# A decoder block on one core: small sums kept together, squares of x out of the head, no low parts on GpSimd after w_o, sums of activations one set later, a last group of 384 and 128 tokens

## The chip, the core and the metric

The kernel runs on one core of one Trainium2 chip. A core has a matrix engine (TensorE, "PE" in the profile; its weight loads are "PEld"), a vector engine (VectorE, DVE), a scalar engine (ScalarE, ACT), GpSimd (POOL), a sync engine that here only issues transfers (SP), and 16 DMA engines. The metric is the device time of one execution in microseconds (us).

## What is computed

One layer of a hybrid decoder on 512 tokens of width 2048, in f32. Six vectors of 2048 (shifts, scales and gates) come from a conditioning vector `c` through `w_ada`; the normed and modulated input goes through one wide matrix `w_in`; two token mixers (latent attention and a gated delta rule) are merged by sigmoid gates; `w_o`, a residual, a second norm, a SwiGLU layer of width 5632, a residual and the last norm follow.

```python
mod = c_act @ w_ada[l] + b_ada[l]
sh_a, sc_a, gt_a, sh_f, sc_f, gt_f = ...
h = _rmsnorm(x, norm_mix[l]) * (1.0 + sc_a) + sh_a
p = h @ w_in[l]
...
mix = (g_a * y_a + g_b * y_b) @ w_o[l]
x = x + gt_a * mix
h = _rmsnorm(x, norm_ffn[l]) * (1.0 + sc_f) + sh_f
gate, up = jnp.split(h @ w_gate_up[l], 2, axis=-1)
x = x + gt_f * ((jax.nn.silu(gate) * up) @ w_down[l])
...
return _rmsnorm(x, final_norm)
```

## The kernel before

**Numbers.** Every f32 operand of a matmul is split into two parts of fewer bits, `hi` (a rounding copy on ACT, L263) and `lo = raw - hi` (a subtraction, L264), and each product is three matmuls: hi·hi, hi·lo, lo·hi (the names `hh`/`hl`, `h2h`/`h2l`, `ah`/`al` are such pairs). So every weight that arrives from memory costs PE three passes, ACT one copy and DVE one subtraction of 128x1024 elements. `lo` usually runs on DVE; for every second unit of some sets (`lo_eng`, `k0 % 4 == 0`) it runs on GpSimd.

**Order.** The work is a list of units. A unit has a load (its raw tile, issued on SP), a split (hi and lo), its matmuls, and a `pre` and `post`. A driver runs the units in order; it splits two units ahead and loads four ahead. After each 12 matmuls (or their weight) it "pumps" the open chains: generators whose steps are put between the matmuls (`yield 2` skips a pump more). PE, POOL and SP keep the order in which the program was written; DVE and ACT are ordered by a scheduler, and an instruction waits for what stands ahead of it on its engine.

**The head.** For k = 0 to 15 (128 rows of `w_in` and of x at a time), `mod_sum` multiplies two 128x1024 tiles of `w_ada` (`rawm`) with c and adds up along the row into `parts` (L435), `mod_columns` turns the two numbers into the scale `s_mix` (three instructions on 128x1 elements, L439, L440, L442), `scaled_h` makes `hh` on ACT and `hl` on DVE from x and the scale, and 24 matmuls of 512 columns follow (`s`, eight PSUM tiles of 128 output rows each). In the same loop `square(k)` squares the tile of x on ACT (L455) and adds it to `x_sum` on GpSimd (`x_sum<-x_sum,sq`). Ahead of the loop PE runs `warm` matmuls whose result is not used.

**The first gate set.** After the head the set `ga` (`ga_...` in the rows) runs in units of 24 matmuls. The chain `x_statistics` puts four one-column matmuls on `x_sum` between them (`xss`, the sums over rows), then a chain of 11 tiny DVE operations for 1/sqrt (`rs`), `diag`, one matmul `rbc` that spreads the result over the partitions, and a copy `r_all`. From then on DVE rescales the tiles of x (L489). Meanwhile DVE works on more `rawm` tiles and the `lo` of each unit.

**The middle.** `w_o` runs in four sets: three over all tokens, the last one (`half_sets`) first for tokens 0 to 255 and then for 256 to 511. When a set is done the residual is added to the tiles `x2[h][q]` (half h of the tokens, rows 256q to 256q+255, as two blocks of 256 columns), they are squared (`squares`), and the squares are added up on GpSimd, but for the last two tiles of a half. `half_rstd` sums them with 12 one-column matmuls (`hss`; the trace has two records for each), takes 1/sqrt, and `hbc` spreads it. `h2_gen` makes the normed halves `h2f` and their parts. The first set of `w_gate_up`, `gu0`, follows the same way in two halves of 8 units, while the second half of `h2` is made beside its first half. `combine` builds sums and differences of the activations (`x5`, `x6`, `x7`, `x3`, L1632, and their parts) for a Strassen product over the 20 later sets; it runs as a chain beside the second half of `gu0`. The set after it, `gu_both(1)`, runs over both halves with 384 matmuls.

**The last group.** The last product of `w_down` (4 of 44 blocks of rows) runs with all weights in place, first for tokens 0 to 255 (8 units of 24 matmuls, each 256 columns wide, names `dnl`), then for tokens 256 to 511. After each unit the residual is added, the tile squared, and scaled by the final norm's column on ACT; after the eighth, `finished(h)` sums the squares (`hss`), takes 1/sqrt, spreads it (`hbc`), multiplies the eight tiles (L1932) and writes them out. For the second half nothing else is left to run beside this.

Of the kernel before, what the change touches and what calls it, by code (L numbers as in the profile page):

```python
# [15 lines left out]
P = 128  # L16
# [155 lines left out]
def block_kernel(ctx: ExitStack, tc: tile.TileContext, a: dict, out):  # L172
# [40 lines left out]
    def bc(ap, n):  # L213
# [223 lines left out]
    def mod_columns(dst, ks, b, norm=None):  # L437

        nc.vector.tensor_reduce(dst[:, ks], parts[:, ks, :], AX.X, ALU.add)  # L439
        nc.vector.tensor_tensor(dst[:, ks], dst[:, ks], b[:, ks], ALU.add)  # L440
        if norm is not None:
            nc.vector.scalar_tensor_tensor(dst[:, ks], dst[:, ks], 1.0, norm[:, ks], op0=ALU.add, op1=ALU.mult)  # L442
# [6 lines left out]
    def square(k):  # L449
# [5 lines left out]
        nc.scalar.activation(s[:], xT[k][:], AF.Square)  # L455
# [4 lines left out]
    def x_statistics():  # L460
        yield 2
# [96 lines left out]
    def head():  # L558
        box = [dict() for _ in range(KT)]
        wait = deque()  # L560
        out_ = [0]
# [33 lines left out]
        for k in range(KT):  # L595
# [5 lines left out]
            square(k)  # L601
# [681 lines left out]
    sums = [[None, []] for _ in range(2)]  # L1283

    def add_gated(h, k, ps, gate):

        d = half_of(x2[h][k // 2], k)
        nc.vector.scalar_tensor_tensor(d, ps, gate[:, k:k + 1], d, op0=ALU.mult, op1=ALU.add)

    def squares(st, tile_, last):  # L1290

        if st[0] is None:
            st[0] = S("xs")
            nc.scalar.activation(st[0][:], tile_[:], AF.Square)
            return
        s = S("sq")
        nc.scalar.activation(s[:], tile_[:], AF.Square)
        if last:
            st[1].append(s)
        else:  # L1300
            nc.gpsimd.tensor_tensor(st[0][:], st[0][:], s[:], ALU.add)

    def half_rstd(st):

        ps = PS("hss")
        sq = [st[0]] + st[1]
        for t in range(2):
            for i, s in enumerate(sq):
                for j in range(2):
                    mm(ps[:, t:t + 1], s[:, 256 * j + P * t:256 * j + P * t + P], ones[:, 0:1], start=i == 0 and j == 0,  # L1310
                       stop=i == len(sq) - 1 and j == 1)
        st[0], st[1] = None, []
        y = token_rstd(ps[:, 0:2], 2, 1.0 / D)
        diag = S("diag")
        for t in range(2):
            nc.vector.tensor_scalar(diag[:, tok(t)], ident, y[:, t:t + 1], None, op0=ALU.mult)
        return diag

    def spread(diag):
        ps = PS("hbc")  # L1320
        mm(ps[:, 0:256], ones[:], diag[:, 0:256], start=True, stop=True)
        return ps[:, 0:256]

    def wo_done(n):
        def done(ps):
            for j in range(4):
# [3 lines left out]
                if j % 2:  # L1330
                    for h in range(2):
                        squares(sums[h], x2[h][k // 2], False)
# [14 lines left out]
    def half_sets(name, loads, x, done):  # L1347
# [3 lines left out]
        def unit(h, k0):  # L1351
# [5 lines left out]
            def split():  # L1357
                box["w"] = halves(box.pop("raw"), 512, 2, nc.gpsimd if k0 % 4 == 0 else None)
# [467 lines left out]
    def ffn():  # L1826
        def gu0():
# [16 lines left out]
            def start():  # L1844
# [3 lines left out]
                xc.append(drv.add(combine()))  # L1848
# [36 lines left out]
        def last_dn():  # L1885
# [11 lines left out]
        def last_unit(h, q):
            box = {}

            def pre():  # L1900
                box["ps"] = PS("dnl")

            def one(j, k, n, wi, xi):
                f = 2 * q + j
                mm(box["ps"][:, 256 * j:256 * j + 256], wl[f // 4, k][wi][:, tok(f % 4)], aT[40 + k][xi][:, 256 * h:256 * h + 256],
                   start=j == 0 and k == 0 and n == 0, stop=k == 3 and n == 2, skip_group_check=True)

            mms = [lambda j=j, k=k, n=n, wi=wi, xi=xi: one(j, k, n, wi, xi)
                   for j in range(2) for k in range(4) for n, (wi, xi) in enumerate(((0, 0), (0, 1), (1, 0)))]

            def post():
                xt = x2[h][q]
                for j in range(2):
                    add_gated(h, 2 * q + j, box["ps"][:, 256 * j:256 * j + 256], gt_ffn)
                squares(sums[h], xt, q > 5)
                for k in (2 * q, 2 * q + 1):
                    nc.scalar.activation(half_of(xt, k), half_of(xt, k), AF.Copy, scale=n_out[:, k:k + 1])
                if q == 7:
                    drv.add(finished(h))
# [102 lines left out]
```

## Time and profile before

| | |
|---|---|
| time, median of 3 runs (lowest, highest) | 2840.56 us (2837.66, 2842.48) |
| the profiled execution: its time, its span, granted TensorE clock | 2836.89 us, 2834.8 us, 0.993 |
| PE busy, share of the span | 2789.9 us, 98% |
| PEld, DVE, ACT, POOL busy | 88%, 66%, 37%, 9% |
| DMA, mean over the span | 174 GB/s |
| after the last `dnl` matmul begins (2816.77) to the end | 18.0 us |

The time is taken on the device from outside the span, so it is 2.1 us longer than the span. The profiled execution is 3.7 us below the median of the runs. A matmul's row in the trace gives its start and a modelled end that overlaps the next ones; how fast PE goes is read from the distance of the starts. "Granted clock" is the share of full speed that the throttle gave PE. With PE busy for 98% of the span, what is left for a change to take are PE's waits, the stretches at half clock, the matmuls themselves, and the tail.

### The profile page before, as it was taken

To read this page: it belongs to the slowest core of one execution; us is meant where nothing else is said; L and a number is where in the kernel's file an instruction comes from. 1 tells how busy PE (TensorE), PEld (TensorE's weight loads), DVE (VectorE), ACT (ScalarE), POOL (GpSimd) and SP (SyncE) were. 2 spreads that over 40 slices of the span, in tenths; PEclk is the share of its full clock that TensorE was granted. 3 is DMA by queue.
4 is the path that set the end of the run, shared out by engine and by line. 5 is a ranking of instruction groups with operands and counts; after the bars stand their busy time and mean duration, and the time that the engine had idled before them with its cause. 6 is when DMAs were issued, how large, how long until landed. Compare 5 with 4: busy or idle time off the path is not lost.

```text
span 2834.8 us, 43579 instructions
## 1 busy us (share of the span) xinstructions
PE 2789.9 (98%) x17082; PEld 2488.0 (88%) x17082; DVE 1860.8 (66%) x3121; ACT 1039.9 (37%) x1429; POOL 244.4 (9%) x284
## 2 busy tenths in 40 slices
PE   8999999999999999999989999999999999999997
PEld 7788788788888888888989999999999998888887
DVE  8875666666868547873475888888888863223234
ACT  4333432543344343222463444444444442112123
POOL 2200011001000000001420000000000140030001
PEclk9999999999999999999999999999999999999998
DMA  9995555545646459884543443444344474363331
GB/s 329 317 374 187 159 178 175 171 149 155 187 142 204 164 182 322 274 291 140 170 136 103 134 137 117 137 134 134 123 132 134 149 251 166 112 212 115 97 104 60
DMA packets 307270, 493.12 MB, mean 174 GB/s; under 512 B 47124, under 2 KB 161972, under 8 KB 306936
## 3 DMA queue, kind: packets, MB, share of 16 engines
q1 hardware_dynamic: 258936, 413.88, 45.2%
q0 software_dynamic: 14256, 46.44, 4.6%
q10 hardware_dynamic: 33872, 30.03, 3.2%
q8 instruction: 133, 2.18, 0.3%
q14 instruction: 73, 0.60, 0.1%
HBM read 438.87 MB, written 51.39 MB: 173 GB/s over the span
## 4 chain that ended last, share of the span: by engine, by line
PE 48%; DVE 1%; DMA 1%; ACT 1%; issue 1%; DVEq 0%; ACTq 0%; SPq 0%
PE m L155 27%; PE dn L155 15%; PE gu L155 3%; PE dnl L155 2%; PE wo L155 1%; DMA raws<-in_w_gate_up_dram 1%; PE hss L155 0%; DMA raw<-in_w_down_dram 0%; ACT h2f L1605 0%; DVE h2l L240 0%; DVE x L1932 0%; ACT hi L263 0%; DVE h2f L1604 0%; ACT h2h L239 0%; DVE lo L264 0%
## 5 line engine op out<-in xcount | busy, mean ns | idle before, releaser
L264 DVE TENSOR_TENSOR lo<-raw,hi 128x1024 fp32r<-128x1024 f32 x322 | 394.7, 1228 | 459.0 <-ACT hi L263 446.6
L263 ACT CAST hi<-raw 128x1024 fp32r<-128x1024 f32 (+1 forms) x338 | 352.1, 1044 | 928.8 <-PE dn L155 254.8
L435 DVE CUSTOM_DVE_ANT_0 rawm<-rawm,cbc 128x1024 f32<-128x1024 f32 x192 | 239.0, 1254 | 146.4 <-DMA rawm<-in_w_mod_dram 145.9
L1701 ACT CAST hi<-sums 128x1024 fp32r<-128x1024 f32 x160 | 167.8, 1049 | 330.4 <-PE m L155 234.5
L155 PE MATMUL m<-h2h,lo 128*128 128x256 f32 x960 | 271.8, 283 | 1.4 <-DVE lo L1702 1.4
L155 PE MATMUL m<-h2h,hi 128*128 128x256 f32 x960 | 271.7, 283 | 0.0
L155 PE MATMUL m<-h2l,hi 128*128 128x256 f32 x960 | 271.7, 283 | 0.0
L1702 DVE TENSOR_TENSOR lo<-sums,hi 128x1024 fp32r<-128x1024 f32 x160 | 195.8, 1224 | 115.2 <-ACT hi L1701 115.2
L155 PE MATMUL dn<-ah,hi 128*128 128x512 f32 x640 | 249.2, 389 | 0.4 <-DVE g L1718 0.4
L155 PE MATMUL dn<-al,hi 128*128 128x512 f32 x640 | 249.0, 389 | 0.0
L155 PE MATMUL dn<-ah,lo 128*128 128x512 f32 x640 | 249.0, 389 | 0.0
L155 PEld LDWEIGHTS m<-h2h,lo 128*128 128x128 f32 x960 | 184.3, 192 | 1.6 <-DVE lo L1702 1.6
L155 PEld LDWEIGHTS m<-h2h,hi 128*128 128x128 f32 x960 | 184.3, 192 | 0.0
L155 PEld LDWEIGHTS m<-h2l,hi 128*128 128x128 f32 x960 | 184.3, 192 | 0.0
L1701 ACT CAST hi<-raws 128x768 fp32r<-128x768 f32 x160 | 133.4, 834 | 122.3 <-PE m L155 88.8
L1702 DVE TENSOR_TENSOR lo<-raws,hi 128x768 fp32r<-128x768 f32 x160 | 152.1, 951 | 5.4 <-ACT hi L1701 5.4
L155 PEld LDWEIGHTS dn<-ah,hi 128*128 128x128 f32 x640 | 120.1, 188 | 26.3 <-DVE g L1718 0.8
L155 PEld LDWEIGHTS dn<-ah,lo 128*128 128x128 f32 x640 | 120.1, 188 | 24.9
L155 PEld LDWEIGHTS dn<-al,hi 128*128 128x128 f32 x640 | 120.1, 188 | 24.7
L1693 DVE TENSOR_TENSOR sums<-sums,raws 128x256 f32<-128x256 f32 x320 | 134.2, 420 | 4.1
L1693 DVE TENSOR_TENSOR sums<-raws 128x512 f32<-128x512 f32 x160 | 109.9, 687 | 10.9 <-DMA raws<-in_w_gate_up_dram 8.2
L155 PE MATMUL wo<-mh,lo 128*128 128x512 f32 (+1 forms) x320 | 111.0, 347 | 2.5 <-POOL lo L155 2.5
(482 smaller groups left out, 7322.7 us busy)
## 6 DMA issues: line engine op xcount, KB each, us to landing
rawm<-in_w_mod_dram SPq DMA_DIRECT2D x192, 512.0 KB, 5.3
raws<-in_w_gate_up_dram SPq DMA_DIRECT2D x320, 256.0 KB, 3.0
raw<-in_w_in_dram SPq DMA_DIRECT2D x144, 512.0 KB, 4.5
raw<-in_w_down_dram SPq DMA_DIRECT2D x88, 512.0 KB, 3.8
raw<-in_w_o_dram SPq DMA_DIRECT2D x40, 512.0 KB, 4.5
rawa<-in_w_in_dram SPq DMA_DIRECT2D x32, 512.0 KB, 4.7
raw<-in_w_gate_up_dram SPq DMA_DIRECT2D x48, 256.0 KB, 3.1
a_dram<-ah POOLq DMA_DIRECT2D x40, 256.0 KB, 2.4
```

What stands on the lines that cost most here:

```text
L155: return self.tc.keep_in_program_order(f(*args, **kwargs))
L263: nc.scalar.copy(hi[:], raw[:])
L264: (lo_eng or nc.vector).tensor_tensor(lo[:], raw[:], hi[:].bitcast(F32), ALU.subtract)
L435: nc.vector.tensor_tensor_reduce(raw, raw, c, 1.0, 0.0, ALU.mult, ALU.add, parts[:, k, half:half + 1])
L1693: add = lambda o, x, y: nc.vector.tensor_tensor(o, x, y, ALU.add)
L1701: nc.scalar.copy(hi[:], src)
L1702: nc.vector.tensor_tensor(lo[:], src, hi[:].bitcast(F32), ALU.subtract)
```

## The change

1. In the head the sums of tile k+1 (`mod_sum`) may only be issued after the last of the three small operations of tile k, so the scheduler cannot put them between those.
2. `square(k)` leaves the head. `x_statistics` now makes the 16 squares itself, two at each pump beside the gate set, before `xss`; the squares keep program order on ACT, the additions stay on GpSimd.
3. `n_out` (the final norm's 16 columns) leaves the first small load and gets a load of its own on SP later.
4. The last set of `w_o` and `gu0` put every `lo` on DVE (before: half of them on GpSimd).
5. `combine` starts with `gu_both(1)` and not in `gu0`, and takes two pumps for each of its steps.
6. `squares` works on segments of tokens; in `w_o`'s last set the last two tiles are added on DVE, so `hss` has 4 matmuls where it had 12.
7. The last group works on tokens 0 to 383 (eight units of 24 matmuls of 384 columns) and then 384 to 511 (four units of 48 matmuls of 128 columns). `finished` for the first part starts two pumps later and gives four pumps between `hss` and `hbc`. The last two tiles' squares stay separate: `hss` of the first part has 18 matmuls, of the last 6.

```diff
 def prepare(k):
-            for half in range(2):
-                use(lambda: mod_sum(box[k], k, half))
-            mod_columns(s_mix, slice(k, k + 1), b_cols[:, 16:32], n_mix)
+            with tc.issue_after(last[0].ins) if last else nullcontext():
+                for half in range(2):
+                    use(lambda: mod_sum(box[k], k, half))
+            last[:] = [mod_columns(s_mix, slice(k, k + 1), b_cols[:, 16:32], n_mix)]
...
-            square(k)
...
     def x_statistics():
-        yield 2
+        for k in range(KT):
+            square(k)
+            if k % 2:
+                yield
+        yield
         ps = PS("xss")
...
     def load_scalars():
+        load(n_out[:], a["out_norm"])
...
-                box["w"] = halves(box.pop("raw"), 512, 2, nc.gpsimd if k0 % 4 == 0 else None)
+                box["w"] = halves(box.pop("raw"), 512, 2)
...
-                    squares(sums[h], x2[h][k // 2], True)
+                    squares(k // 2, HALF[h], nc.vector)
...
                 for name in ("x3", "x6", "x7", "x5"):
                     comb[q][name] = hilo(res.pop(name)[:], name)
-                yield
+                yield 2
...
-                              cols=slice(256 * h, 256 * h + 256), lo_eng=True, alone=True)
+                              cols=slice(256 * h, 256 * h + 256), alone=True)
...
-                xc.append(drv.add(combine()))
...
-        yield from gu_both(1)
+        yield from with_pre(gu_both(1), lambda: xc.append(drv.add(combine())))
...
-            for h in range(2):
-                for q in range(8):
-                    yield last_unit(h, q)
+            for q in range(8):
+                yield last_unit(FIRST, [2 * q, 2 * q + 1], 1)
+            for q in range(0, 8, 2):
+                yield last_unit(LAST, [2 * q + i for i in range(4)], 4)
+
+        FIRST, LAST = [(0, 0, 256), (1, 0, 128)], [(1, 128, 128)]
...
+            mms = [lambda i=i, k=k, m=m, wi=wi, xi=xi: one(i, k, m, wi, xi)
+                   for i in range(len(fs)) for k in range(4) for m, (wi, xi) in enumerate(((0, 0), (0, 1), (1, 0)))]
...
+                for q in range(fs[0] // 2, fs[-1] // 2 + 1):
+                    for seg in segs:
+                        squares(q, seg, nc.gpsimd if q < 6 else None)
...
+        def finished(segs):
+            more = segs is FIRST
+            if more:
+                yield 2
+            diag = part_rstd(segs)
+            if more:
+                yield 4
+            r = spread(*diag)
```

**DVE at the start, before.** `lo` is the first unit's; L439, L440 and L442 make the first scale `s_mix`, `rawm` (L435) are the sums of the next tile.

```order
L264 TENSOR_TENSOR lo_186<-raw_149,hi_185 128x1024
L439 TENSOR_REDUCE s_mix<-parts 128x1
L435 ISA rawm_151,parts<-rawm_151,cbc 128x1024
L435 ISA parts 128x1
L440 TENSOR_TENSOR s_mix<-s_mix,columns 128x1
L435 ISA rawm_153,parts<-rawm_153,cbc 128x1024
L435 ISA parts 128x1
L442 SCALAR_TENSOR_TENSOR s_mix<-s_mix,columns 128x1
L439 TENSOR_REDUCE s_mix<-parts 128x1
```

After, the same place:

```order
L264 TENSOR_TENSOR lo_187<-raw_150,hi_186 128x1024
L439 TENSOR_REDUCE s_mix<-parts 128x1
L440 TENSOR_TENSOR s_mix<-s_mix,columns 128x1
L442 SCALAR_TENSOR_TENSOR s_mix<-s_mix,columns 128x1
L435 ISA rawm_152,parts<-rawm_152,cbc 128x1024
L435 ISA parts 128x1
L488 SCALAR_TENSOR_TENSOR hl_183<-xT_148,s_mix,hh_182 128x512
L435 ISA rawm_154,parts<-rawm_154,cbc 128x1024
L435 ISA parts 128x1
```

The three small operations of the first tile now follow each other directly; the two sums of the next tile stand behind them.

**DVE in the gate set, before.** The end of the 1/sqrt chain (`rs`), `diag` for the matmul `rbc`, and the `lo` of the set's fifth unit:

```order
L435 ISA rawm_1033,parts<-rawm_1033,cbc 128x1024
L435 ISA parts 128x1
L232 SCALAR_TENSOR_TENSOR rs_1077<-rs_1077,rs_1075 128x4
L233 SCALAR_TENSOR_TENSOR rs_1076<-rs_1077,rs_1076 128x4
L231 TENSOR_TENSOR rs_1077<-rs_1076 128x4
L232 SCALAR_TENSOR_TENSOR rs_1077<-rs_1077,rs_1075 128x4
L233 SCALAR_TENSOR_TENSOR rs_1076<-rs_1077,rs_1076 128x4
L468 TENSOR_SCALAR diag_1089<-kc,rs_1076 128x128 x4
L264 TENSOR_TENSOR lo_1101<-raw_1038,hi_1100 128x1024
L435 ISA rawm_1044,parts<-rawm_1044,cbc 128x1024
L435 ISA parts 128x1
L435 ISA rawm_1095,parts<-rawm_1095,cbc 128x1024
```

After, the end of the same chain (`lo_1189` is the eighth unit's):

```order
L264 TENSOR_TENSOR lo_1189<-raw_1142,hi_1188 128x1024
L231 TENSOR_TENSOR rs_1213<-rs_1212 128x4
L435 ISA rawm_1148,parts<-rawm_1148,cbc 128x1024
L435 ISA parts 128x1
L232 SCALAR_TENSOR_TENSOR rs_1213<-rs_1213,rs_1211 128x4
L435 ISA rawm_1181,parts<-rawm_1181,cbc 128x1024
L435 ISA parts 128x1
L233 SCALAR_TENSOR_TENSOR rs_1212<-rs_1213,rs_1212 128x4
L472 TENSOR_SCALAR diag_1225<-kc,rs_1212 128x128 x4
L264 TENSOR_TENSOR lo_1249<-raw_1186,hi_1248 128x1024
L435 ISA rawm_1192,parts<-rawm_1192,cbc 128x1024
L435 ISA parts 128x1
```

Before, `diag` stood ahead of the `lo` of the set's fifth unit; now it stands ahead of that of the ninth. On PE `xss` moved from the start of the third unit to the middle of the sixth, and `rbc` from the end of the third to the middle of the seventh.

**ACT in the gate set, after.** The squares of x (L455), the copies `hi` of the units, and `r_all`:

```order
L455 ACTIVATE sq_1084<-xT_446 128x512
L455 ACTIVATE sq_1087<-xT_491 128x512
L263 CAST hi_1096<-raw_1046 128x1024
L455 ACTIVATE sq_1114<-xT_536 128x512
L455 ACTIVATE sq_1117<-xT_581 128x512
L455 ACTIVATE sq_1132<-xT_626 128x512
L455 ACTIVATE sq_1135<-xT_671 128x512
L263 CAST hi_1144<-raw_1094 128x1024
L455 ACTIVATE sq_1162<-xT_716 128x512
L455 ACTIVATE sq_1165<-xT_761 128x512
L263 CAST hi_1188<-raw_1142 128x1024
L263 CAST hi_1248<-raw_1186 128x1024
L476 COPY r_all_89<-rbc_1266 128x512
```

The last six squares stand behind the copy `hi` of the sixth unit (`hi_1096`), and the very last two behind that of the seventh (`hi_1144`); before, ACT had only `hi` copies, eight copies of results and `r_all` in this set.

**DVE in `gu0`, before.** `h2f` and `h2l` make the second half's normed activations, L1632 and `x3l` to `x5l` are `combine`:

```order
L1632 TENSOR_TENSOR x_2044_12195<-h2f_12186,h2f_12026 128x512
L1632 TENSOR_TENSOR x_2045_12197<-h2f_11660,x_2044_12195 128x512
L1632 TENSOR_TENSOR x_2046_12199<-h2f_11660,h2f_12026 128x512
L1632 TENSOR_TENSOR x_2047_12201<-x_2045_12197,h2f_11820 128x512
L264 TENSOR_TENSOR lo_12328<-raw_12131,hi_12327 128x1024
L240 TENSOR_TENSOR x3l_12204<-x_2047_12201,x3h_12203 128x512
L240 TENSOR_TENSOR x6l_12220<-x_2045_12197,x6h_12219 128x512
L1604 SCALAR_TENSOR_TENSOR h2f_12242<-x_1766_10260,s_ffn,hbc_12024 128x256 x2
L264 TENSOR_TENSOR lo_12423<-raw_12227,hi_12422 128x1024
L240 TENSOR_TENSOR h2l_12248<-h2f_12242,h2h_12247 128x512
L240 TENSOR_TENSOR x7l_12252<-x_2046_12199,x7h_12251 128x512
L240 TENSOR_TENSOR x5l_12268<-x_2044_12195,x5h_12267 128x512
```

After, the same unit of `gu0`:

```order
L1621 SCALAR_TENSOR_TENSOR h2f_12176<-x_1764_10258,s_ffn,hbc_12014 128x256 x2
L264 TENSOR_TENSOR lo_12238<-raw_12081,hi_12237 128x1024
L240 TENSOR_TENSOR h2l_12182<-h2f_12176,h2h_12181 128x512
L1621 SCALAR_TENSOR_TENSOR h2f_12216<-x_1766_10262,s_ffn,hbc_12014 128x256 x2
L264 TENSOR_TENSOR lo_12278<-raw_12121,hi_12277 128x1024
L240 TENSOR_TENSOR h2l_12222<-h2f_12216,h2h_12221 128x512
L1621 SCALAR_TENSOR_TENSOR h2f_12256<-x_1768_10266,s_ffn,hbc_12014 128x256 x2
L264 TENSOR_TENSOR lo_12318<-raw_12161,hi_12317 128x1024
L240 TENSOR_TENSOR h2l_12262<-h2f_12256,h2h_12261 128x512
L1621 SCALAR_TENSOR_TENSOR h2f_12296<-x_1770_10270,s_ffn,hbc_12014 128x256 x2
L264 TENSOR_TENSOR lo_12349<-raw_12201,hi_12348 128x1024
```

The rows of `combine` are gone from here; they stand behind the twenty-odd rows that end `gu0`, between the units of the next set. The `lo` of each unit, half of which were on GpSimd, now all stand here.

More of the change, by code (lines that the diff above doesn't have):

```diff
@@ L1281, in load_x2, with add_gated, view @@
                      a["xT"][256 * q:256 * q + 256, 256 * h:256 * h + 256].rearrange("(k p) n -> p k n", p=P))
-    sums = [[None, []] for _ in range(2)]
-    def add_gated(h, k, ps, gate):
-        d = half_of(x2[h][k // 2], k)
+    sums = {}
+    def add_gated(h, k, ps, gate, c0=0):
+        d = half_of(x2[h][k // 2], k)[:, c0:c0 + ps.shape[1]]
         nc.vector.scalar_tensor_tensor(d, ps, gate[:, k:k + 1], d, op0=ALU.mult, op1=ALU.add)
[L1290 to L1295, printed above, removed]
+    def view(tile_, seg):
+        return tile_[:].rearrange("p (k n) -> p k n", k=2)[:, :, seg[1]:seg[1] + seg[2]]
@@ L1296, in squares @@
+    def squares(q, seg, eng):
         s = S("sq")
-        nc.scalar.activation(s[:], tile_[:], AF.Square)
-        if last:
-            st[1].append(s)
-        else:
-            nc.gpsimd.tensor_tensor(st[0][:], st[0][:], s[:], ALU.add)
-    def half_rstd(st):
+        st = sums.setdefault(seg, [])
+        nc.scalar.activation(view(s, seg), view(x2[seg[0]][q], seg), AF.Square)
+        if st and eng is not None:
+            eng.tensor_tensor(view(st[0], seg), view(st[0], seg), view(s, seg), ALU.add)
+        else:
+            st.append(s)
@@ L1305, in half_rstd, with part_rstd @@
+    def part_rstd(segs):
         ps = PS("hss")
[L1306 to L1313, printed above, removed]
+        n = sum(seg[2] for seg in segs) // P
+        todo = []
+        for i in range(max(len(sums[seg]) for seg in segs)):
+            t0 = 0
+            for seg in segs:
+                if i < len(sums[seg]):
+                    v = view(sums[seg][i], seg)
+                    todo += [(t0 + t, v[:, j, tok(t)]) for t in range(seg[2] // P) for j in range(2)]
+                t0 += seg[2] // P
+        for i, (t, v) in enumerate(todo):
+            mm(ps[:, t:t + 1], v, ones[:, 0:1], start=i == 0, stop=i == len(todo) - 1, skip_group_check=True)
+        for seg in segs:
+            del sums[seg]
+        y = token_rstd(ps[:, 0:n], n, 1.0 / D)
@@ L1314, in half_rstd, with spread @@
         diag = S("diag")
-        for t in range(2):
+        for t in range(n):
             nc.vector.tensor_scalar(diag[:, tok(t)], ident, y[:, t:t + 1], None, op0=ALU.mult)
-        return diag
-    def spread(diag):
+        return diag, n * P
+    def spread(diag, n):
         ps = PS("hbc")
-        mm(ps[:, 0:256], ones[:], diag[:, 0:256], start=True, stop=True)
-        return ps[:, 0:256]
+        mm(ps[:, 0:n], ones[:], diag[:, 0:n], start=True, stop=True)
+        return ps[:, 0:n]
@@ L1892, in last_dn @@
                     yield weights.pop(0)
-            for h in range(2):
-                for q in range(8):
-                    yield last_unit(h, q)
[L1897 to L1919, printed above, removed]
-            return Unit(mms=mms, pre=pre, post=post)
@@ new lines, in finished @@
+        def finished(segs):
[5 more added lines that the diff above has]
+                yield 4
+            r = spread(*diag)
+            o = 0
+            for seg in segs:
+                h, c0, n = seg
+                rs = r[:, o:o + n].unsqueeze(1).broadcast_to([P, 2, n])
+                o += n
+                for q in range(8):
+                    v = view(x2[h][q], seg)
+                    nc.vector.tensor_tensor(v, v, rs, ALU.mult)
+                    (load if more or q % 2 == 0 else nc.scalar.dma_start)(
+                        out[256 * q:256 * q + 256, 256 * h + c0:256 * h + c0 + n].rearrange("(k p) n -> p k n", p=P), v)
+                    if more:
+                        yield
```

63 lines of the change are left out of this document (39 added, 24 removed).

## The prediction

> **What bounds the kernel now.** First the page's engine table, then the waits of PE, then windows of the stages that the change touches. A change of under 0.2% (5.7 us) is about what a measurement of this kernel cannot tell from none.
>
> The page's busy times, and the first of PE's waits (total, times, longest):
>
> ```profile
> PE 2789.9 (98%) x17082; PEld 2488.0 (88%) x17082; DVE 1860.8 (66%) x3121; ACT 1039.9 (37%) x1429; POOL 244.4 (9%) x284
> ...
> PE gu L155 <- ACT h2h L239: 5.9, 2, 5.0
> PE hbc L155 <- DVE diag L1316: 5.0, 3, 2.8
> PE s L155 <- ACT hh L483: 4.4, 1, 4.4
> PE rbc L155 <- DVE diag L468: 3.4, 1, 3.4
> ...
> PE wo L155 <- POOL lo L155: 2.5, 1, 2.5
> ```
>
> PE is the bound at 98%, so only its waits, its half-clock stretches, its own work and the tail count. All five waits are touched by the change. Windows (span, then PE, PEld, DVE, ACT, POOL busy with counts, granted clock, DMA share, GB/s):
>
> ```profile
> 14.60:21.40 6.80, 5.64 (x12) 4.08 (x13) 6.16 (x17) 3.86 (x5) 0.00 (x0) 0.50 1.01 375
> 15.76:35.76 20.00, 20.00 (x75) 15.93 (x76) 18.80 (x30) 8.65 (x12) 3.08 (x2) 0.86 0.97 360
> 105.80:127.20 21.40, 18.01 (x84) 14.59 (x82) 15.04 (x37) 4.85 (x6) 1.65 (x4) 1.00 0.95 335
> 127.20:130.70 3.50, 3.50 (x9) 2.40 (x8) 3.50 (x7) 1.64 (x2) 0.00 (x0) 0.51 0.98 336
> 135.00:160.00 25.00, 25.00 (x112) 20.70 (x111) 23.38 (x37) 7.60 (x10) 2.16 (x4) 1.00 0.95 322
> 1417.50:1424.30 6.80, 6.80 (x34) 6.80 (x33) 3.22 (x13) 2.34 (x4) 2.35 (x1) 0.50 0.52 164
> 1428.00:1477.00 49.00, 42.50 (x325) 41.60 (x324) 40.03 (x54) 30.79 (x49) 12.04 (x5) 0.93 0.45 141
> 1468.70:1475.50 6.80, 6.50 (x28) 6.21 (x29) 4.43 (x8) 1.96 (x4) 0.00 (x0) 0.50 0.36 117
> 1477.00:1524.00 47.00, 47.00 (x393) 46.93 (x392) 23.67 (x35) 16.50 (x25) 2.74 (x5) 1.00 0.28 90
> 2791.90:2794.50 2.60, 2.60 (x26) 2.60 (x25) 0.48 (x1) 0.00 (x0) 0.00 (x0) 1.00 0.00 0
> ```
>
> Three things to see. A wait of PE is often followed by a stretch at clock 0.50 that costs half its length again. DVE is as good as full in the head (18.80 of 20) and in the gate set (23.38 of 25), but half idle in `gu_both(1)` (23.67 of 47). In `gu0`'s second half (1428 to 1477) PE is busy for 42.5 of 49 us, with DVE at 40.
>
> **1. Head.** The rows of the first tile:
>
> ```profile
> 12.38 0.15 DVE L439 TENSOR_REDUCE s_mix<-parts 128x1 f32<-128x2 f32 x1
> 12.44 1.21 DVE L435 CUSTOM_DVE_ANT_0 rawm<-rawm,cbc 128x1024 f32<-128x1024 f32 x1
> 14.80 0.15 DVE L442 SCALAR_TENSOR_TENSOR s_mix<-s_mix,columns 128x1 f32<-128x1 f32 x1
> 14.99 0.72 ACT L483 ACTIVATE hh<-xT,s_mix 128x512 fp32r<-128x512 f32 x1 [3.78 <-DVE s_mix L442]
> 15.76 0.79 PE L155 MATMUL s<-hh,hi 128*128 128x512 f32 x1 [4.38 <-ACT hh L483]
> ```
>
> Two `rawm` sums lie between L439 (12.38) and L442 (ends 14.95). Now the three small ones follow each other: 12.38 + two steps of about 0.2 + 0.15 = 12.95, so `hh` and the first matmul come 2.0 us earlier, at 13.8. PE's idle time before it falls from 4.4 to 2.4 us, so the half-clock stretch from 14.6 (12 matmuls in 6.8 us) shrinks or goes: worth 0 to 2.4 us, I take 1.5. The head gives **-3.5** (-2 to -4.4), if supply keeps up; with DVE freed of what follows, it should. The extra load of 16 columns is one small transfer among 97% busy DMA engines: nothing that shows.
>
> **2. Squares in the gate set.** What a GpSimd addition does to DVE:
>
> ```profile
> 27.39 1.79 POOL L155 TENSOR_TENSOR x_sum<-x_sum,sq 128x512 f32<-128x512 f32 x1 [19.34 <-ACT sq L455]
> 27.95 2.31 DVE L435 CUSTOM_DVE_ANT_0 rawm<-rawm,cbc 128x1024 f32<-128x1024 f32 x1
> L155 POOL TENSOR_TENSOR x_sum<-x_sum,sq 128x512 f32<-128x512 f32 x15 | 25.7, 1713 | 68.7 <-ACT sq L455 68.6
> ```
>
> The same DVE instruction takes 1.21 alone and 2.31 beside the addition: 1.1 us per addition, 15 x 1.1 = 16.5 us. They move from the head into the gate set, whose DVE is just as full, four per unit. Its rows:
>
> ```profile
> 126.59 1.47 PE L155 MATMUL rbc<-diag,ones 128*128 128x512 f32 x2 [3.39 <-DVE diag L468]
> 131.21 1.22 DVE L264 TENSOR_TENSOR lo<-raw,hi 128x1024 fp32r<-128x1024 f32 x1
> 133.65 1.06 ACT L263 CAST hi<-raw 128x1024 fp32r<-128x1024 f32 x1 [3.14 <-DVE parts L435]
> 135.96 1.22 DVE L264 TENSOR_TENSOR lo<-raw,hi 128x1024 fp32r<-128x1024 f32 x1
> ```
>
> Before, this stage lost about 5.6 us of waiting around `rbc` plus 1.8 at half clock (127.2 to 130.7). DVE made a unit in 4.75 us (131.21 to 135.96), PE needs 24 x 0.223 = 5.4 (25 us for 112): a gain of 0.65 per unit, no cover for 4.4. The last two squares stand on ACT behind the seventh unit's `hi`, which waits for DVE (before: 133.65). I date that copy: the sixth unit's `lo`, 131.21 before, moves by +12 (11 additions), -3.2 (the 1/sqrt chain now comes later), -1.4 (two rescalings too), -1.9 (head's gain less three result copies now ahead of the first `hi`): 136.7; the copy 2.4 later, 139.1; two squares and two additions, `xss` at about 144.5. PE without any stall would be at its place at about 132. So 12.5 us are lost there; then `rbc` waits some 2 us for the 1/sqrt chain, which now has a `lo` and four sums in it, and half clock follows for 1 us more than the starved PE would notice. 15.5 against 7.4: **+8**. Bounds: +1 if the additions fall into the idle time of DVE (it has 6.4 us from 105.8 to 127.2), +20 if an addition blocks DVE for all its 1.71 us (15 x 1.71 = 25.7, less 5.6 of slack and cover). I take the middle since the measured pair says 1.1.
>
> **3. The middle.**
>
> - `lo` on DVE: 16 x 1.22 = 20 us more work (8 units of `w_o`'s last set, 8 of `gu0`), against 16 times at least the 1.1 of blocking that a shorter GpSimd operation made: about even for DVE, and the wait `wo<-POOL lo` of 2.5 goes (**-2.6** with the clock step behind it).
> - `combine` out of `gu0`: 16 subtractions and 16 `lo` parts of 0.68 = 22 us of DVE leave a stage with 40 of 49 busy. The `h2h` that PE waited for stood behind two `lo` and two of `combine`'s parts. The waits of 5.9 and their restarts are about 7.8, the half clock from 1468.7 costs 3: **-10.8**. They go to `gu_both(1)`, where DVE then has 23.7 + 22 = 46 of 47 us at most (part of it ran there already). If that cover is too thin, PE waits there: +1 to +11, taken as +1.5.
> - `hss` with 8 records where there were 24 (26 records in 2.6 us): two halves save 2 x 1.6, and the second one's half clock from 1417.5 (3 us) with its `hbc` wait of 0.9 probably goes; an added DVE addition on the path costs about 1: **-6**.
>
> Together **-18**, of which I count -17 since a next wait always stands behind the one removed (range -10 to -20).
>
> **4. The last group.** The only rows for matmuls of 384 and 128 columns are the attention scores':
>
> ```profile
> 879.88 0.34 PE L155 MATMUL sc<-knl,qnh 128*128 128x384 f32 x1
> 880.05 0.34 PE L155 MATMUL sc<-knh,qnl 128*128 128x384 f32 x1
> 872.78 0.28 PE L155 MATMUL sc<-knl,qnh 128*128 128x128 f32 x1
> 872.89 0.28 PE L155 MATMUL sc<-knh,qnl 128*128 128x128 f32 x1
> 2784.83 0.28 PE L155 MATMUL dnl<-al,wlh 128*128 128x256 f32 x1
> 2784.95 0.28 PE L155 MATMUL dnl<-ah,wll 128*128 128x256 f32 x1
> ```
>
> Starts lie 0.17, 0.11 and 0.12 apart. Before: 384 x 0.120 = 46.1. After: 192 x 0.173 + 192 x 0.111 = 33.2 + 21.3 = 54.5, **+8.4**: 128 columns cost almost what 256 do. `hss` of the first part grows to 36 records (+1.2), its `hbc` wait (1.5) goes with four pumps; a half-clock stretch after so many one-column matmuls is likely (24 of them had one at 1417.5 and none at 2791.9): +2.5 of at most 3.4.
>
> The Trainium skill ("TensorE: Matmul & The Clock Gate", Back-to-back issue gap) gives about 81 ns per 128-column matmul in a stream with weight loads, and 131 ns for 512 columns. By it the last part would take 192 x 0.081 = 15.6, estimated, so 5.8 less. The rows here show 0.11, and 0.223 for 512 columns, so I go by the rows. The same page (LDWEIGHTS) has 107 ns for 128 columns of weights, which is the spacing seen.
>
> The tail, now over 128 tokens and not 256:
>
> ```profile
> 2817.09 0.88 DVE L1288 SCALAR_TENSOR_TENSOR x<-dnl,gt_ffn,x 128x256 f32<-128x256 f32 x2 [2.00 <-PE dnl L155]
> 2818.06 0.63 ACT L1297 ACTIVATE sq<-x 128x512 f32<-128x512 f32 x1 [1.31 <-DVE x L1288]
> 2819.63 1.16 PEld L155 LDWEIGHTS hss<-ones,sq 128*128 128x128 f32 x8
> 2823.68 1.22 PE L155 MATMUL hbc<-diag,ones 128*128 128x256 f32 x2 [2.81 <-DVE diag L1316]
> 2825.01 4.87 DVE L1932 TENSOR_TENSOR x<-x,hbc 128x512 f32<-128x512 f32 x8 [1.38 <-PE hbc L155]
> DMA packets 2177, 2.11 MB, mean 118 GB/s; under 512 B 128, under 2 KB 2176, under 8 KB 2176
> ```
>
> After the square `hss` keeps 4 records of 16 (-1.5), square and `diag` halve (-0.5), `hbc` halves (-0.4), eight multiplications of 4.87 become about 2.8 (-2.0); the output halves in bytes at the same number of rows, so the last transfers end -0.5 to -1.5 sooner. **-5.3** (-4 to -6). The last group: 8.4 + 1.2 - 1.5 + 2.5 - 5.3 = **+5.3** (+3 to +9).
>
> **Sum.** -3.5 + 8 - 17 + 5.3 = -7.2 us. The profiled execution of 2836.9 would become 2829.7. It lies 3.7 below the median of the runs, so against that median, 2840.6, I forecast 2833.4.
>
> **Rivals.**
> - *The gate set eats it all (slower).* If an addition holds DVE for its whole 1.71 us, and the late `xss` and `rbc` starve PE on top, the stage loses 28 against 7.4 before: +21, and the sum is +6 or more: 2847. It decides from 1.4 us per addition on. For it: DVE has no idle time at all from 127.2 to 130.7, and ACT's order ties the last squares to a unit's `hi` that needs DVE. Against: the measured 1.1.
> - *`combine` only moves its waits.* `gu_both(1)` would lose the 10.8 that `gu0` gains: -7.2 + 9.3 = +2: 2842.7, no change. For it: 46 of 47 us of DVE. Against: PE there needs only one `lo` of 1.22 per 5.75 us, which is split two units ahead.
> - *The squares cost nothing new.* With DMA 95% busy and DVE idle for 6.4 us of the set's first 21.4, the additions may fall into gaps that DMA makes: +1 for +8, -14.2 in all: 2826.4.
> - *128-column matmuls run at their own width*, half of 0.120: 192 x 0.060 = 11.5, the last group 9.8 cheaper: 2823.6. Against: the `sc` rows. The skill's 81 ns would give 2827.6.
>
> **How the numbers follow.** The forecast's case 0.42, squares free 0.18, gate set eats it 0.15, `combine` moves 0.20, narrow matmuls quick 0.05. Faster by over 0.2% (under 2834.9): two thirds of the first, all of the second and the last: 0.50. Slower (over 2846.2): the third and a fifth of the fourth: 0.20. Within: 0.30. The first case alone spans 2827 to 2840. The range 2823 to 2847 leaves out the worst of the gate set and the sum of all good ends.
>
> **What would show it.** `s` at about 13.8 us; waits `xss<-POOL x_sum` of several us and an `rbc` wait; `rawm` rows of 2.3 between 115 and 150 us; no `wo<-POOL lo` and no wait of `gu` over 1 us, `gu0` at 46 to 47 us per 384 matmuls, DVE near full in `gu_both(1)`; `dnl` starts 0.173 and 0.111 apart; about 12.5 us from the last `dnl` to the end. The forecast is wrong if the gate set ends at the same distance from its start as before, if `gu` waits move one set on, or if the 128-column starts are not 0.11 apart.

## The result: 16.6 us slower; the last group alone lost 25 us

The changed kernel takes 2857.6 us (median of 4 runs, 2854.9 to 2859.5), the kernel before 2841.0 beside it: ratio 1.0059, 95% interval 1.0042 to 1.0077. The forecast was 2833.4, faster, with a range that ended at 2847. The profiled execution took 2859.5, its span 2857.7, that is 22.9 more than the one before. (The profiled execution after is the slowest of its four, the one before is faster than all four beside it, so the traces show some 6 us more than the medians.)

The engines, PE's waits and the clock by slices, from the page and the view of waits, after:

```profile
PE 2811.1 (98%) x17050; PEld 2510.7 (88%) x17050; DVE 1877.2 (66%) x3165; ACT 1042.9 (36%) x1453; POOL 209.9 (7%) x273
...
PEclk9999999999999999999999999999999999999996
...
PE xss L155 <- POOL x_sum L155: 11.8, 1, 11.8
PE hbc L155 <- DVE diag L1331: 6.8, 3, 2.6
PE k L155 <- DVE lo L264: 3.7, 1, 3.7
...
PE s L155 <- ACT hh L487: 2.4, 1, 2.4
...
PE hss L155 <- DVE sq L1308: 1.9, 1, 1.9
```

The waits of `gu` and of `wo` are gone, `s` has 2.4 where it had 4.4, `rbc` has none; new is `xss` with 11.8. The last slice's clock is 0.6 where it was 0.8. A page of busy times hides the main loss: PE is at 98% again, since matmuls at half clock count as busy.

Where the 22.9 us arose, from the starts of each stage's matmuls in the two traces:

| stage | before | after | difference |
|---|---|---|---|
| to the end of the head's `s` | 105.6 | 102.7 | -2.8 |
| gate set `ga`, to its end (`ga` to `q`) | 94.1 | 104.1 | +10.0 |
| up to `w_o` (a longer wait of `k`, 526 us) | 1028.6 | 1031.0 | +2.3 |
| `w_o` with the first half's `hss` | 182.5 | 180.1 | -2.4 |
| `gu0`, first half of tokens (30.6, 30.5), second (33.0, 23.0) | 63.6 | 53.6 | -10.0 |
| `gu_both(1)` | 46.4 | 46.1 | -0.4 |
| Strassen sets and `w_down` up to the last group | 1244.9 | 1246.2 | +1.3 |
| last group, first to last `dnl` | 50.8 | 77.8 | +27.0 |
| from there to the end | 18.0 | 16.0 | -2.1 |

Windows of the last group after (columns as before: span; PE, PEld, DVE, ACT, POOL busy; clock; DMA share; GB/s), and two rows of PE:

```profile
2797.29:2801.26 3.97, 3.97 (x38) 3.97 (x37) 0.74 (x2) 2.32 (x6) 0.00 (x0) 1.00 0.00 0
2807.60:2817.60 10.00, 10.00 (x48) 10.00 (x49) 3.43 (x18) 2.11 (x6) 0.72 (x1) 0.50 0.01 2
2819.20:2841.70 22.50, 22.50 (x108) 22.50 (x107) 9.67 (x24) 4.23 (x12) 2.92 (x4) 0.50 0.34 111
...
2801.26 6.24 PE L155 MATMUL hss<-ones,sq 128*128 128x1 f32 x36
2817.64 1.59 PE L155 MATMUL hbc<-diag,ones 128*128 128x384 f32 x2
```

The 128-column stream begins at full clock, 38 matmuls in the first 3.97 us (two of them at the edges of the window). The first part's `hss` follows, and from 2802.94 to the end the clock is 0.50: 48 matmuls in 10.0 us, 108 in 22.5, which is 0.21 each and not 0.111. Everywhere else in these two traces a half-clock stretch ahead of the tail ends after 3.4 or 6.8 us, or 13.7 in the starved gate set. This one lasts for the 54.8 us that remain.

### The profile page after: what moved, and what is told of

It reads as the page before. It is cut to its first block, busy times and chain, and to the rows that moved or that the text cites. A ratio compares the mean times of both kernels' runs of the same rounds, so it can differ in the third digit from the quotient of the medians.

```text
span 2857.7 us, 43631 instructions
## 1 busy us (share of the span) xinstructions
PE 2811.1 (98%) x17050; PEld 2510.7 (88%) x17050; DVE 1877.2 (66%) x3165; ACT 1042.9 (36%) x1453; POOL 209.9 (7%) x273
## 4 chain that ended last, share of the span: by engine, by line
PE 94%; DVE 2%; DMA 2%; ACT 1%; issue 1%; POOL 0%; ACTq 0%; SPq 0%; DVEq 0%; POOLq 0%
PE m L155 27%; PE dn L155 15%; PE gb L155 6%; PE wo L155 6%; PE v L155 4%; PE z L155 3%; PE gu L155 3%; PE ya L155 3%; PE yb L155 3%; PE q L155 3%; PE s L155 3%; PE dnl L155 2%; PE k L155 2%; PE ga L155 2%; PE qk L155 2%; PE ckv L155 2%
## 5 line engine op out<-in xcount | busy, mean ns | idle before, releaser
L264 DVE TENSOR_TENSOR lo<-raw,hi 128x1024 fp32r<-128x1024 f32 x338 | 418.3, 1240 | 452.8 <-ACT hi L263 439.4
L435 DVE CUSTOM_DVE_ANT_0 rawm<-rawm,cbc 128x1024 f32<-128x1024 f32 x192 | 241.2, 1269 | 153.6 <-DMA rawm<-in_w_mod_dram 153.2
L155 PE MATMUL wo<-mh,hi 128*128 128x512 f32 (+1 forms) x320 | 111.2, 347 | 0.0
```

The costliest lines, as they stand in the source:

```text
L155: return self.tc.keep_in_program_order(f(*args, **kwargs))
L264: (lo_eng or nc.vector).tensor_tensor(lo[:], raw[:], hi[:].bitcast(F32), ALU.subtract)
L435: nc.vector.tensor_tensor_reduce(raw, raw, c, 1.0, 0.0, ALU.mult, ALU.add, parts[:, k, half:half + 1])
```

## The experiments

**The last group.** Four kernels, each the changed one with one edit.

*a1_halves*: 256 and 256 tokens again.

```diff
-                yield last_unit(FIRST, [2 * q, 2 * q + 1], 1)
-            for q in range(0, 8, 2):
-                yield last_unit(LAST, [2 * q + i for i in range(4)], 4)
+                yield last_unit(FIRST, [2 * q, 2 * q + 1], 2)
+            for q in range(8):
+                yield last_unit(LAST, [2 * q, 2 * q + 1], 2)
-        FIRST, LAST = [(0, 0, 256), (1, 0, 128)], [(1, 128, 128)]
+        FIRST, LAST = [(0, 0, 256)], [(1, 0, 256)]
```

> The changed kernel with its last group back at 256 and 256 tokens (8 + 8 units of 24 matmuls of 256 columns); everything else of the change stays. Theory (the last group's half clock is the loss): matmuls of 256 columns keep the array full at half clock as well, so the clock comes back to 1.00 within 7 us of `hss`; the last group takes 51 us and not 78, the tail 2 us more: about 2833, below the kernel before. Rival (the loss sits in the other parts and the clock at the end is only a symptom): over 2845.

Measured: 2829.4 us (2827.3 to 2833.4), 0.9968 [0.9955, 0.9980] of the kernel before: faster than that, and 26 us less than the changed kernel by the two ratios (0.0091 x 2840). Its `hss` drops the clock as well, but 256 columns bring it back in one stretch:

```profile
2789.20:2792.70 3.50, 3.50 (x19) 3.50 (x18) 2.52 (x13) 0.76 (x2) 0.09 (x1) 0.51 0.00 0
2792.70:2809.00 16.30, 16.30 (x137) 16.25 (x136) 9.07 (x18) 8.41 (x17) 6.39 (x5) 1.00 0.39 131
```

*a4_late_hss*: the first part's chain 12 pumps later.

```diff
             if more:
-                yield 2
+                yield 12
             diag = part_rstd(segs)
```

> The changed kernel, with the chain of the first part started 12 pumps later and not 2, so that 150 matmuls of 128 columns run before any one-column matmul. Theory A (one-column matmuls drop the clock): the clock is 1.00 for these 16 us, starts 0.111 apart, and falls only at the late `hss`; the first part's end then lies in the tail: about 2850. Theory B (the stream drops it by itself): 0.50 within 3.4 to 7 us of the first 128-column matmul, ahead of any `hss`: 2860 or more.

Measured: 2857.0 (2852.9 to 2858.3), 1.0057 [1.0042, 1.0072]. The time lies between A's 2850 and B's 2860 and decides nothing, as the first part's multiplications now lie in the tail; the clock answers the question:

```profile
2797.50:2813.30 15.80, 15.80 (x144) 15.80 (x144) 3.24 (x12) 6.19 (x18) 2.19 (x3) 1.00 0.00 1
2814.70:2828.00 13.30, 13.30 (x63) 13.30 (x64) 2.47 (x14) 0.49 (x2) 0.64 (x1) 0.50 0.00 0
...
2813.45 6.75 PE L155 MATMUL hss<-ones,sq 128*128 128x1 f32 x36
```

Narrow matmuls keep full clock for 15.8 us, 144 in a row. `hss` begins at 2813.45, the clock falls at 2814.6, and the same stream then stays at 0.50. So theory B falls: the stream does not drop the clock, `hss` does.

*a3_push*: 24 matmuls of 512 columns behind `hss`.

```diff
             diag = part_rstd(segs)
             if more:
+                push = PS("push")
+                for _ in range(24):
+                    mm(push[:], wl[0, 0][0][:, tok(0)], aT[40][0][:], start=True, stop=True)
                 yield 4
```

> The changed kernel, with 24 matmuls of 512 columns, whose result is not used, put behind `hss` of the first part (10 us at half clock, 5.5 at full). Theory A (128 columns keep the clock that they find): the wide matmuls release the throttle after 3.4 to 6.8 us, and the rest of the 128-column stream runs at 0.111: saves some 13 us and costs 8: 2850 to 2854. Theory B (the stream drops the clock itself): the clock comes back and falls again within 7 us: 2860 to 2865. Theory C (the low clock at the end has another cause than how busy the array is): no return, 2866 to 2868.

Measured: 2849.6 (2847.3 to 2855.6), 1.0041 [1.0028, 1.0055]: 8 us less in the medians and 5 by the ratios than without this extra work (the intervals overlap), just below A's 2850 to 2854.

```profile
2805.30:2811.50 6.20, 6.20 (x16) 4.94 (x17) 2.46 (x14) 0.00 (x0) 0.00 (x0) 0.50 0.00 0
2815.50:2831.70 16.20, 16.20 (x144) 15.94 (x143) 10.55 (x28) 6.35 (x18) 3.66 (x5) 1.00 0.48 156
```

The wide matmuls bring the clock back after 6 us, and the narrow stream behind them (144 in 16.2 us) holds it to the tail. Theory C falls too: the same code at the same place runs at either clock, depending on what ran before it.

*a2_few_hss*: the last two squares added on DVE, 12 records of `hss` and not 36.

```diff
-                        squares(q, seg, nc.gpsimd if q < 6 else None)
+                        squares(q, seg, nc.gpsimd if q < 6 else nc.vector)
```

> The changed kernel, with the last two tiles' squares added on DVE too, so that `hss` of the first part has 12 records of one column and not 36. Theory A (one-column matmuls drop the clock, and a stream of 128 columns keeps whatever clock it finds): with 1.3 us of them and not 5 no window is idle enough, the clock stays 1.00, the 128-column starts stay 0.111 apart: about 2832 to 2835. Theory B (a stream of 128 columns drops the clock by itself, since its weight loads leave the array half idle): the clock falls to 0.50 within 7 us of the stream's start all the same: 2850 to 2855.

Measured: 2852.5 (2850.9 to 2856.5), 1.0046 [1.0031, 1.0061]: in time this is B's figure, and A's figure is missed.

```profile
2799.90:2801.20 1.30, 1.30 (x14) 1.30 (x13) 0.00 (x0) 0.00 (x0) 0.00 (x0) 1.00 0.00 0
2803.70:2833.40 29.70, 29.70 (x137) 29.09 (x137) 11.29 (x31) 6.34 (x18) 3.65 (x5) 0.50 0.26 85
```

With a4 beside it, A holds, but its figure for a window that is idle enough was wrong: 1.3 us of one-column matmuls among narrow ones were enough for the drop, and not in the profiled run alone: the granted clock of the four runs is 0.985 to 0.987, near the changed kernel's 0.984 to 0.985 and not a1's 0.991 to 0.993. (Among 256-column matmuls 0.9 us of them were not, e2 below.)

**Head, gate set, `combine`.** Four kernels on top of a1_halves (2829.4).

*d1_xss*: `xss` 36 matmuls later.

```diff
             if k % 2:
                 yield
-        yield
+        yield 4
         ps = PS("xss")
```

> On the last group of 256 and 256 tokens (2829.4): `xss` stands 36 matmuls (8.2 us at full clock) later on PE, in the seventh unit's second half; nothing else moves but what follows it. Theory A (PE waits 11.8 us at `xss` for a chain of 14 GpSimd additions of 2.06 us, while the weights' parts are ready): PE works through most of that time, the wait falls to 2 to 4 us and the time to 2821 to 2824. Theory B (DVE, slowed by the same additions, is the limit, and `xss` only the place where it shows): PE waits for `lo` instead, or for `rbc` later; less than 3 us gained, 2827 or more.

Measured: 2828.9 (2824.3 to 2830.1), 0.9964 [0.9951, 0.9977]: no difference from a1 that the runs can tell. In its profile the wait of `xss` fell and the gate set took 4.2 us less:

```profile
PE xss L155 <- POOL x_sum L155: 4.8, 1, 4.8
...
PE ga L155 <- DVE lo L264: 1.2, 2, 0.8
PE rbc L155 <- DVE diag L472: 1.0, 1, 1.0
```

Part of A's and part of B's: 7 us less at `xss`, 1.8 of them back at `ga` (0.4 in a1) and `rbc` (none in a1). That the rest did not reach the time fits a half-clock stretch of 6.8 us at 521.9, where a1 had none; nothing here shows that it would come in each run.

*d2_sqhead*: the squares back in the head, the tie kept.

```diff
-        for k in range(KT):
-            square(k)
-            if k % 2:
-                yield
-        yield
+        yield 2
         ps = PS("xss")
...
+            square(k)
             u, head_units[k] = head_units[k], None
             u.pre()
```

> On the last group of 256 and 256 tokens (2829.4): the squares of x and their additions are back in the head, `xss` at its old place; the small sums stay tied. If moving the squares is what cost 10 us in the gate set, and the tie alone gave the head's 2.8 us: the head ends at 102.7 to 103.5, the gate set as before the change, about 2819.5. Rival (the head's gain came from the squares leaving it): the head ends at 105 or later, 2822 or more. Second rival (the gate set is slow for another reason, such as the set's three result copies ahead of its first `hi`): no gain, 2829.

Measured: 2819.9 (2819.2 to 2821.0), 0.9935 [0.9918, 0.9951]: 9.5 us less than a1, as expected. In the profiles the head ends at 104.4, 1.6 us later than in a1 and between the expected 103.5 and the rival's 105: part of the head's gain did come from the squares. The gate set takes 13.8 less; `rbc`, which lost 3.4 us before the change, now waits 1.1:

```profile
PE s L155 <- ACT hh L483: 3.8, 1, 3.8
...
PE rbc L155 <- DVE diag L468: 1.1, 1, 1.1
```

*d4_comb0*: `combine` in `gu0` again, at its old pace (in `gu0`'s start `xc.append(drv.add(combine()))` and not at `gu_both(1)`; `yield` for `yield 2`).

> On the last group of 256 and 256 tokens (2829.4): `combine` is back in `gu0`'s second half, one pump for each step. If it was `combine` on DVE that made PE wait in `gu0`: the wait of `h2h` at about 5 us is back, with a half-clock stretch, 8 to 11 us slower: 2837.5 to 2840. Rival (the low parts on GpSimd made that wait, and they stay away here): within 3 us, 2829 to 2832.

Measured: 2837.5 (2833.0 to 2843.1), 8.1 more than a1. `gu0`'s second half takes 27.9 us for 23.0, with a wait of `h2h` again, 2.6 us and not 5, and clock 0.94:

```profile
1447.40:1474.80 27.40, 24.50 (x190) 24.10 (x189) 26.52 (x38) 16.91 (x25) 0.00 (x0) 0.94 0.56 173
...
PE gu L155 <- ACT h2h L239: 2.6, 1, 2.6
```

So `combine` made that wait, and 4.9 of the 9.1 us between the two spans lie where it was; the rest lies in half-clock stretches and waits elsewhere, outside the edit.

*d6_untie*: without the tie (the `with tc.issue_after...` line of `prepare` removed).

> On the last group of 256 and 256 tokens (2829.4): the small sums are not tied, the squares stay out of the head. If the tie gives the 2.2 us of the first matmul and nothing more: first `s` at 15.8 again, 2831 to 2833. Rival (without the squares the scheduler finds the same order, or the head gets the time back from DVE's freed time): the same as with the tie, 2829.4.

Measured: 2833.3 (2827.8 to 2838.1), 3.9 more than a1 (the intervals overlap). The first `s` starts at 15.2 (a1 13.7), PE's wait for it is 5.2 us, the head ends at 105.4 (102.8). Without the tie, taking the squares out thus gains 0.2 us of the head's 105.6; with the tie and the squares back in (d2) the head gains 1.2. The 2.8 us need both.

**Single terms on d2_sqhead (2819.9).** Kernels of this group are compared by their ratios to the kernel before on their own chip (d2: 0.9935).

*e1_poollo*: half of the low parts on GpSimd again (`nc.gpsimd if k0 % 4 == 0` in `half_sets`, `lo_eng=True` in `gu0`).

> On the version with the last group of 256 and 256 tokens and the squares of x back in the head (2819.9): half of the low parts of the last set of `w_o` and of `gu0` are on GpSimd again. If they were worth what the prediction said: PE waits some 2.5 us for a GpSimd `lo` in `w_o` again, and DVE, without `combine` in `gu0`, has room for the blocking: 2822 to 2824. Rival (the blocking of DVE, 1.1 us for each, also makes PE wait in `gu0`): 2826 or more. Second rival (the low parts' place never mattered): 2820.

Measured: 2826.7, 0.9955 [0.9939, 0.9972], 5.7 us more than d2 by the ratios (0.0020 x 2840; the intervals overlap a little). `wo<-POOL lo` is back with 2.5 us, `w_o` takes 1.5 longer and `gu0`'s first half 33.0 for 29.9, its `hss` waiting 5.0 us for DVE:

```profile
PE hss L155 <- DVE sq L1305: 5.0, 1, 5.0
...
PE wo L155 <- POOL lo L155: 2.5, 1, 2.5
...
1417.02 2.37 POOL L155 TENSOR_TENSOR lo<-raw,hi 128x1024 fp32r<-128x1024 f32 x1 [5.08 <-ACT hi L263]
1417.49 2.44 DVE L1305 TENSOR_TENSOR sq<-sq,sq 128x512 f32<-128x512 f32 x1
```

The rival's time came in the median (by the ratios it would be 2825.6), and the profile has its mechanism: the DVE addition that `hss` waits for took 2.44 us beside a GpSimd `lo`, where d2's took 0.68, and `gu0`'s first half lost more (3.1 us) than `w_o` with its direct wait (1.5). The kernel before had no DVE addition in that place, so this price belongs to the two changes together.

*e3_oldhss*: `hss` after `w_o` with 24 records again (`squares(k // 2, HALF[h], None)` for `nc.vector`).

> On the same version (2819.9): the last two tiles' squares of each half after `w_o` stay separate, as before the change, so `hss` there has 24 records and not 8. Expected by the prediction's term of 6: 3.2 to 3.6 for the records, and a longer stretch at half clock behind the second half's `hss`: 2824 to 2826. Rival (the clock falls there with 8 records too, so only the records count): 2822 to 2823.

Measured: 2824.7, 0.9947 [0.9932, 0.9962], 3.4 us more by the ratios, intervals overlapping. In the profile `w_o` and `gu0` together lose 0.3 us against d2 (the end of `wo` +1.3, the end of `gu` back -1.0, with no half-clock stretch in `gu0` where d2 had one at 1417.7); the other 6.7 of the 7.0 between the spans lie in front of and behind them. Inconclusive: the term is not worth 6 in its place.

*e2_few*: a2's edit on this version.

> On the same version (2819.9): the last two tiles' squares of each half of the last group are added on DVE, so that `hss` has 8 records and not 24. The first half's `hss` (2.7 us of one-column matmuls) drops the clock for 3.4 us there; with 0.9 us it should stay at 1.00: -1.8 for the records and -1.7 for the clock; the tail loses a DVE addition (0.7) and gains 8 records (0.9 to 1.7): 2815 to 2817. Rival (the clock falls all the same, or the addition on GpSimd's sum comes late): 2818 to 2820.

Measured: 2818.0 (2815.5 to 2821.6), 0.9923 [0.9908, 0.9938]; 3.4 us less than d2 by the ratios, the intervals overlapping. In the profile the last group's matmuls end 3.3 us sooner, with no half clock from `hss` to the tail, and the tail takes 0.6 longer:

```profile
2777.60:2797.60 20.00, 20.00 (x168) 19.95 (x166) 12.63 (x34) 10.56 (x21) 6.47 (x5) 1.00 0.32 107
```

*e4_best*: e2, and more pumps for the chains after `w_o`.

```diff
-        yield
+        yield 3 if h else 1
         diag = part_rstd([HALF[h]])
-        yield 2
+        yield 4
```

> On the same version (2819.9): as e2_few, and after `w_o` the chains get more pumps: two more ahead of the second half's `hss` (PE waits 1.9 us there for a DVE addition) and two more between `hss` and `hbc` of both halves (PE waits 2.0 and 2.4 us for the 1/sqrt chain), with two half-clock stretches behind. If PE finds other work in that time: -6 for the waits, -2 to -3.4 for the clock, and e2_few's 3: 2808 to 2812. Rival (`h2` becomes late instead and PE waits for it in `gu0`): 2815 to 2818.

Measured: 2814.3 (2810.9 to 2816.0), 0.9908 [0.9893, 0.9922] of the kernel before: the lowest median here (its interval overlaps e2's), 26 us below the one before, and 43 below the changed one by the ratios. `w_o` takes 3.7 and `gu0`'s first half 2.9 us less than in d2, at clock 1.00. The expected 2808 to 2812 was not reached.

## Why the prediction was wrong, step by step

**The step that failed** is in part 4: "a half-clock stretch after so many one-column matmuls is likely (...): +2.5 of at most 3.4". Of the 30.1 us between the forecast's -7.2 and the measured +22.9 in the traces, 19.6 arose in the last group with its tail. That the stretch comes was right; that it ends was taken from the stretches of the trace before, all of which were ended by matmuls of 256 or 512 columns. 156 of the 192 narrow matmuls (48 and 108 in the two windows) ran at 0.21 instead of 0.11: 156 x 0.102 = 15.9 us. `hss` had 20 of its records at half clock (+2.0). So some 17.9 us came where +2.5 stood.

Why the narrow stream does not bring the clock back can be narrowed down from the starts. At half clock 256-column matmuls start 0.213 us apart (a1) and 512-column ones 0.427 (a3), twice as much: the columns set the pace. 128-column ones start 0.213 apart as well, and so do the one-column `hss`; what these two share is the load of 128 columns of weights. At full clock the starts lie 0.111 apart for 128 columns and for one, and 0.227 for 512 (a3). So at either clock the narrow stream passes about half of the columns that wide matmuls pass in the same time. That this half is what neither frees the clock nor drops it fits all traces here, but no run varied it: it is inferred, not shown.

The tail gave 2.1 us where I expected 5.3. The eight multiplications (2.73 us for 4.87), `diag` and `hbc` came about as priced. `hss` did not: its last 8 records took 2.05 us at half clock, the 16 before 2.13, most of it at full clock. And what stands behind the last multiplication took 6.1 us for 5.0, and not less: 13 writes lie there, where I counted eight.

```profile
2849.34 5.62 SPq L155 DMA_DIRECT2D out_dram<-x  x9
...
2849.68 2.41 ACTq L1969 DMA_DIRECT2D out_dram<-x  x4
```

`finished` puts one pump behind each of the first part's 16 writes. Eleven of them were issued ahead of the last part; the other five, whose tiles DVE had multiplied by 2827.8, stand on SP behind the last part's. The last write of the last part landed at 2854.55, the last of these five at 2856.70: about 2.1 us of the tail, an estimate from the two landings.

The widths themselves were priced right as long as the clock was full. The range looked at the gate set for the slow side and at this only for 3.4 us. The rival of 0.060 per narrow matmul did not come: 144 in 15.8 us (a4) are 0.11 each. Nor did the 81 ns of the Trainium skill ("TensorE: Matmul & The Clock Gate", Back-to-back issue gap).

The Trainium skill ("TensorE: Matmul & The Clock Gate", Part 1) says the gate opens after about 3.4 us of sustained activity. The runs agree for wide matmuls (3.4 us in a1, 6.2 from the first wide one in a3) and differ for the narrow stream: PE is busy without a gap in the window from 2819.2, for 22.5 us, and the clock stays at 0.50. That instructions follow each other without a gap is thus not enough.

**Head, -3.5: -2.8**, by the tie and the missing squares together (d6, d2): with the tie, the head ends at 102.1 to 103.5 in the seven traces without the squares and at 104.3 to 106.3 in the five with them. The first `s` came at 13.56, forecast 13.8; the half clock fell from 6.8 to 3.4 us.

**Gate set, +8: +10.0**, the right size by a partly wrong road, so in part by luck. I had `xss` at 144.5 (it came at 145.54), held up by ACT's order. ACT had finished the squares at 132.4; its copies `hi` waited for the weights' transfers there and not for DVE. ACT's order only kept GpSimd idle for 9.27 us, until 116.6; from then on the hold-up was GpSimd itself. Its row and one of DVE's, after:

```profile
116.61 28.87 POOL L155 TENSOR_TENSOR x_sum<-x_sum,sq 128x512 f32<-128x512 f32 x14 [9.27 <-ACT sq L455]
119.36 2.30 DVE L435 CUSTOM_DVE_ANT_0 rawm<-rawm,cbc 128x1024 f32<-128x1024 f32 x1
...
116.60:145.50 28.90, 17.18 (x76) 13.89 (x74) 25.09 (x20) 11.91 (x18) 27.85 (x14) 0.86 0.79 256
```

14 additions back to back at 2.06 us each, while every DVE operation of 128x1024 from 117.1 to 141.6 takes 2.3 for 1.22; the two additions behind that, with DVE idle, took 1.26. The two engines block each other, and a saturated DVE makes an addition dearer than the 1.71 that it took on average in the head. The 1.1 us on the DVE side was right, the price of the other side was missing. `rbc` did not wait. "The gate set eats it all" did not come, "the squares cost nothing new" neither.

**Middle, -17: -12.8.** `gu0` took 53.6 us for its 384 matmuls, not 46 to 47. Its second half gave 10.0 against 10.8, and `combine` was only part of its cause: alone it costs 4.9 there (d4), the GpSimd low parts alone nothing (23.0 in e1), both together 10.0. Nothing came back in `gu_both(1)` (46.1 us at DVE 35 of 46), so that rival fell. The low parts: `w_o` -2.4 with the first half's `hss` in it, against -2.6 for them alone; e1 shows that they can be worth more than that where DVE blocking counts. The records of `hss`, -6: nothing in `gu0`'s first half (30.6 and 30.5). Fewer records let PE arrive earlier at two other waits, `hss` for the added DVE addition (1.9) and `hbc` for the 1/sqrt chain (2.2), and the half clock only fell from 6.8 to 3.4 us. e4 got 2.9 us there by moving the two waits.

**Not in the sum: +2.3 and +1.3.** Waits near 526 us (`k`) and 2317 us (`m`) that the change does not touch cost more or less from one trace to the next, since a wait of 2 to 4 us sometimes brings a half-clock stretch and sometimes not: a1, with the same code there, had the stretch at 567 and none at 526 or 2318.

## What to carry to other kernels

Price a narrower matmul at both clocks, and ask whether the stream behind a drop can bring the clock back: here the 128-column stream could not, and a single pause before it cost the rest of the stream, not one window. Busy shares hide this; read the granted clock of each stretch, or the distance of the starts. When work on GpSimd moves beside a saturated DVE, price both sides of the block and where its result is waited for. Where a chain takes a pump for each step, count the pumps that are left: steps that do not fit land in the tail. And after taking a wait away, date the next instruction on the same chain before booking the gain.

## What the hardware showed that was not expected

- A stream of 128-column matmuls with a weight load each is neither a drop nor a release: it kept 1.00 for 15.8 us (a4) and 16.2 us (a3), and 0.50 for 13.3 us (a4) and 29.7 us (a2). 16 matmuls of 512 columns ended such a state in 6 us (a3).
- 1.3 us of one-column matmuls inside that stream were enough to drop the clock (a2); 0.9 us inside a 256-column stream were not (e2).
- In every trace here the clock changes only at times that lie whole steps of 3.41 us apart (before: the falls at 14.61, 127.25, 1417.49 and 1468.69 are 33, 378 and 15 steps apart), and where a group of one-column matmuls lies between these times matters. In the trace before, 24 of them (2.6 us, among 256-column matmuls) dropped the clock with 2.1 us in one step (from 1415.41) and did not with 1.1 and 1.5 in two (from 2791.91). Of a2's 1.3 us, 0.95 lay in the step that ended with the fall; of e2's 0.9, 0.7 lay in one. So these are single cases, not thresholds.
- A GpSimd addition of 128x512 took 2.1 to 2.2 us beside a full DVE and 1.26 beside an idle one (at 142.9 and 144.2 in the trace after); a DVE operation of 128x1024 took 2.3 us beside it and 1.22 alone.
